# Row factors of the first blocks, side units, late finishes, query loads and the last scaling of a hybrid encoder layer: five placements changed

## The chip, the cores and the metric

The kernel runs on one core of one Trainium2 chip. The core has a matmul engine (PE, with its weight loads PEld), a vector engine (DVE), an activation engine (ACT), a general engine (POOL) and a queue engine (SP); DMAs are issued by SP, POOL and ACT. The metric is device microseconds of one execution, and a kernel's time is the median of its runs.

## The reference

One layer works on a sequence of 4096 rows of width 1024, all in float32. Cut to what matters:

```
hn   = rms_norm(x, norm_w)
proj = hn @ w_in                     # q,k,v,o,z and gates of group A; q,k,v,z of group B
qk_a = silu(conv5(qk_a) + conv_b)    # depthwise, centred
# group A, 4 heads x 128: a scan over chunks of 128 rows, once forward, once backward
#   s   = (q k^T) * exp(dmat - m);  num = s v + w * (q C);  den = sum(s) + w * (q n)
#   h   = num / max(|den|, exp(-m));  C = decay * C + (w k)^T v
h    = sigmoid(o) * (h_fwd + h_bwd)
h    = h * rsqrt(mean(h*h) + eps) * mhn_w * silu(z)
# group B, 8 query heads / 2 kv heads x 64: attention within |i-j| <= 128, bias table, sink
y_b  = attention(q, k, v) * silu(z_b)
out  = rms_norm(x + concat(h, y_b) @ w_out, final_norm_w)
```

## The kernel before, in words

The program has four stages that follow each other on PE. Matmuls take each float32 operand as a rounded high part and a low part, so a product is three matmuls (low times high, high times low, high times high). Products with the gate and the output weights are formed with seven block products instead of eight, which needs sums of blocks of rows and of weights made ahead.

`pass1` (lines 161 to 678) goes over 16 blocks of 256 rows. Each block's row factor 1/rms is worked out from the rows (ACT squares, DVE, then a power on POOL) and stored to the small DRAM tensor `rs_d`, 128 values of 4 bytes per store, by `keep_rows` (line 177, issued by POOL). For blocks 3 to 15, `spread` (line 260, issued by SP) reads a block's 256 factors back as a row on all partitions, `scale_raw` (line 265, POOL) multiplies the transposed input with them, ACT casts the high part (line 274) and POOL subtracts (line 275). Blocks 0 to 2 are normalised from their rows directly (`norm_now`, `norm_both`, `norm`); their factors are only kept in `KEPT` and stored for pass 2. The attention of group B runs interleaved: scores, transposes, and the weighted sum `op` (line 424), evicted to the one buffer `ab` by ACT (line 436) and DVE (line 437) and stored to `at_d` (line 439). Near the end of pass 1 a last list of pieces carries hooks at given positions; hook 1 held the stores of `KEPT`.

`pass2` goes over eight blocks `b` of 512 rows, from 7 down to 0. For each block it makes the values (`v2p`, line 999), then keys (parts `m` 4 to 7) and queries (`m` 0 to 3) of the four heads (`up`, line 1026); each part is copied by ACT, convolved with one ACT and four DVE instructions (lines 1043, 1045) and finished by a tanh on ACT, a DVE product (lines 1049, 1050) and a store. A finish can be put off into `c.late[m]` and called later in the stream. Keys are transposed (`ktp`, line 1091, psum tag "b" with two buffers), copied by ACT and DVE (lines 1093, 1094), and multiplied with the weighted values (`kv`, lines 151 to 153). The split input of the next block, eight tiles `xb` of 514 KB, is loaded by SP (line 861) while the last query part of the present one runs. Beside this run "side units" that prepare the sums for the seven-product form: `punit` (input blocks 0 to 2, which needs the row factors in `rs_d`), `sunit` and `wunit` (weights). Each has four steps: load, sums, low part, store. `side(b)` is called 16 times in a block, eight times in the value projections and eight times in the key projections, and starts unit `z` at given calls with steps 0, 3, 5 and 6 calls later.

`pass3` walks over 32 chunks. Per chunk PE does 42 matmuls of a gate stream (`P`, line 1332) with the scan's own work in fixed places between: `heads` (`num`, lines 1468, 1469), `scores` (`S`, line 1444) of the next chunk, the transpose of the finished chunk (`yout`, line 1503). DVE evicts the products (`o`, `z`, lines 1313 to 1323), and does `W` times `q` (line 1458), the decayed scores `E` (line 1446) and, last of a chunk, four products with the factor `ss` (line 1496), which POOL's power (line 1494) delivers. The chunk's inputs are loaded by SP two chunks ahead (`load_scan`); the gate stream's raw sums are loaded by `raw` (line 1271).

`tail` makes the output projection and the final norm.

The order on PE is the order in which the program is written. On the other engines and in the DMA queues a planner orders instructions by a simulated time line and by priority; `issue_after` (helper `behind`) puts an instruction behind a given one of its engine. Each engine executes its list in order, so an instruction that waits holds up all behind it. Tiles come from pools with a fixed number of buffers: `xtile` has 14 of 4 KB per partition, `c.slot` has 20 of about 2 KB.

Of the kernel before, what the change touches and what calls it, by code (L numbers as in the profile page):

```python
# [20 lines left out]
NH = 4  # L21
# [139 lines left out]
def pass1(c):  # L161
    nc, tc, A = c.nc, c.tc, c.A
    NB = 16
    with ExitStack() as es:
# [446 lines left out]

        norm_now(0)
# [58 lines left out]
        hooks.append((1, lambda: [keep_rows(b, i, r) for (b, i), r in KEPT.items()]))  # L671
# [199 lines left out]
def pass2(c):  # L871
    nc, tc, A = c.nc, c.tc, c.A
    with ExitStack() as es:
# [78 lines left out]
        def punit(b):  # L952
            T = {}

            def load():
                T["x"] = [xtile(c, [128, 4, 256], F32, f"xs{b}_{h}") for h in range(2)]
                T["r"] = c.slot([128, 256], F32, f"rs{b}")
                for h in range(2):
                    nc.gpsimd.dma_start(T["x"][h], A["xt"][b, :, 4 * h:4 * h + 4, :])
                nc.gpsimd.dma_start(T["r"], c.rs_d[b].partition_broadcast(128))  # L960

            def scale():
                for x in T["x"]:
                    nc.vector.tensor_tensor(out=x, in0=x, in1=T["r"].unsqueeze(1).broadcast_to([128, 4, 256]), op=ALU.mult)

            def store():
                for h in range(2):
                    nc.gpsimd.dma_start(c.xo_d[b, h], T["x"][h])

            return load, scale, lambda: block_sums(nc.vector, T["x"]), store  # L970
# [7 lines left out]
        def side(b):  # L978
# [6 lines left out]
            for z, u in enumerate(SIDE[b][1]):  # L985
                for d, f in zip((0, 3, 5, 6), u):
                    if ((0, 2, 5, 8) if b > 3 else (0, 4, 8))[z] + d == t:
                        f()
# [22 lines left out]
        def qkproj(b, m):  # L1011
# [6 lines left out]
            def unit(lo, hi, k, j):  # L1018
# [38 lines left out]
                if m == 7 or m == 0 and 0 < b < 7 or m == 3 and b:  # L1057
# [79 lines left out]
        for b in range(7, -1, -1):  # L1137
# [45 lines left out]
            if 0 < b < 7:  # L1183
# [79 lines left out]
def gate_stream(c):  # L1263
# [23 lines left out]
    def pair(j):  # L1287
# [49 lines left out]
        def ahead(i):  # L1337
            if i < 6:
                split(j, i + 1)
            plan = [(2, whole, j, 5), (3, whole, j, 6), (4, whole, j + 1, 0), (5, raw, j + 1, 3), (6, raw, j + 1, 2)]  # L1340
# [65 lines left out]
def pass3(c):  # L1406
    nc, tc, A = c.nc, c.tc, c.A
    with ExitStack() as es:
# [3 lines left out]
        Ls, OZ, TZ, HS, NUM = c.Ls, c.OZ, c.TZ, {}, {}  # L1412
# [47 lines left out]
        def heads(n, h):  # L1460
# [34 lines left out]
            for h in range(NH):  # L1495
                nc.vector.scalar_tensor_tensor(hs[:, h, :], hs[:, h, :], ss[:, h:h + 1], zs[:, h, :],
                                               ALU.mult, ALU.mult)
# [30 lines left out]
        for n in range(NCH):  # L1528
            m = n + 1
            with behind(c, c.rawd if n == 0 else None):  # L1530
                load(n + 2, ("cc", "e", "w", "q"))
# [17 lines left out]
            if m < NCH:  # L1549
                pieces.append(lambda: (scores(m), load(n + 2, ("k",))))  # L1550
                pieces.append(lambda: None)
            else:
                pieces += [lambda: None] * 6 + [lambda: yout(n)] + [lambda: None] * 2
# [350 lines left out]
```

## Time and profile before

| what | value |
|---|---|
| runs (us) | 2209.07, 2199.22, 2204.91; median 2204.91 |
| profiled execution | 2198.4 us, its span 2196.7 us |
| PE busy | 2129.6 us (97% of the span) |
| DVE, ACT, POOL busy | 1552.0, 1139.0, 715.5 us |
| mean granted PE clock | 0.994 |
| bytes moved | 460.72 MB, mean 210 GB/s |

In the profile, busy times are sums of instruction durations on an engine, and a line such as "PE a L1 <- DVE b L2: 5.0, 3, 2.1" says that PE's instruction of line 1 waited for DVE's of line 2, 5.0 us in total, 3 times, 2.1 us at the longest. A row of the time line gives start, duration, engine, line, operation, output and inputs, count, and in brackets the engine's idle time before it with what ended it. A row of windows gives the stretch, each engine's busy time with the instruction count, the granted clock, the share of the DMA engines and GB/s.

### The profile page before, as it was taken

To read this page: it belongs to the slowest core of one execution; us is meant where nothing else is said; L and a number is where in the kernel's file an instruction comes from. 1 tells how busy PE (TensorE), PEld (TensorE's weight loads), DVE (VectorE), ACT (ScalarE), POOL (GpSimd) and SP (SyncE) were. 2 spreads that over 40 slices of the span, in tenths; PEclk is the share of its full clock that TensorE was granted. 3 is DMA by queue.
4 is the path that set the end of the run, shared out by engine and by line. 5 is a ranking of instruction groups with operands and counts; after the bars stand their busy time and mean duration, and the time that the engine had idled before them with its cause. 6 is when DMAs were issued, how large, how long until landed. Compare 5 with 4: busy or idle time off the path is not lost.

```text
span 2196.7 us, 35248 instructions
## 1 busy us (share of the span) xinstructions
PE 2129.6 (97%) x12034; PEld 1843.2 (84%) x12034; DVE 1552.0 (71%) x3195; ACT 1139.0 (52%) x2764; POOL 715.5 (33%) x1055
## 2 busy tenths in 40 slices
PE   7899999999989999999999999999999999999998
PEld 7899999999888787788888788888888788888886
DVE  6677777778876775767765777777777543867776
ACT  6688888878644443444443455555555321333333
POOL 3565766653014233312410232332232111112222
PEclk9999999999999999999999999999999999999999
DMA  9665655533227546634666988888779998667765
GB/s 263 170 179 156 199 151 190 175 114 116 71 84 256 191 151 220 230 127 144 224 201 237 334 260 259 266 267 280 252 253 308 335 356 288 185 179 191 193 187 149
DMA packets 285762, 460.72 MB, mean 210 GB/s; under 512 B 23180, under 2 KB 151180, under 8 KB 284045
## 3 DMA queue, kind: packets, MB, share of 16 engines
q1 hardware_dynamic: 246016, 323.94, 46.4%
q0 software_dynamic: 39328, 134.25, 20.2%
q8 instruction: 95, 1.56, 0.3%
q14 instruction: 87, 0.70, 0.1%
q10 hardware_dynamic: 236, 0.27, 0.1%
HBM read 305.20 MB, written 153.17 MB: 209 GB/s over the span
## 4 chain that ended last, share of the span: by engine, by line
PE 64%; DMA 13%; DVE 8%; issue 7%; ACT 4%; POOL 3%; SPq 1%; POOLq 0%; ACTq 0%; DVEq 0%
PE up L1026 14%; PE P L1332 9%; PE qp L547 7%; PE v2p L999 5%; DMA xr<-x 5%; PE op L424 4%; PE tp L410 3%; PE zbp L151 3%; PE sp L379 3%; PE zbp L153 3%; PE zbp L152 3%; DMA xb<-xT_d 2%; PE o L1670 2%; PE num L1469 2%; PE num L1468 2%
## 5 line engine op out<-in xcount | busy, mean ns | idle before, releaser
L1332 PE MATMUL P<-wt,op 128*128 128x512 f32 x1344 | 364.1, 407 | 6.2 <-DVE o L1313 4.4
L1026 PE MATMUL up<-xb,w 128*128 128x512 f32 x1344 | 334.4, 396 | 0.0
L1670 PE MATMUL o<-wo,yo 128*128 128x512 f32 (+1 forms) x1356 | 312.7, 393 | 0.0
L1670 PEld LDWEIGHTS o<-wo,yo 128*128 128x128 f32 x1356 | 253.3, 188 | 59.5
L1026 PEld LDWEIGHTS up<-xb,w 128*128 128x128 f32 x1344 | 245.0, 188 | 48.5
L1332 PEld LDWEIGHTS P<-wt,op 128*128 128x128 f32 x1344 | 237.0, 189 | 53.1 <-issue 9.1
L1045 DVE SCALAR_TENSOR_TENSOR qk<-U,cw,qk 128x512 f32<-128x512 f32 x256 | 194.8, 761 | 82.5 <-ACT qk L1043 72.6
L547 PE MATMUL qp<-xT,wqb 128*128 128x256 f32 x1536 | 242.8, 288 | 0.1
L547 PEld LDWEIGHTS qp<-xT,wqb 128*128 128x128 f32 x1536 | 214.6, 190 | 8.4 <-DVE wqb L320 0.5
L413 DVE TENSOR_TENSOR pt<-tp,pt 128x512 fp32r<-128x512 f32 x188 | 129.6, 690 | 65.9 <-ACT pt L412 65.2
L999 PE MATMUL v2p<-w,xb 128*128 128x512 f32 x672 | 161.8, 401 | 8.7 <-DMA xb<-xT_d 7.2
L390 ACT ACTIVATE s<-s,NG 128x320 f32<-128x320 f32 (+1 forms) x256 | 142.2, 556 | 50.9 <-DVE NG L382 49.5
L382 DVE CUSTOM_DVE_ANT_0 s<-sp,G,nsink 128x320 f32<-128x320 f32 (+1 forms) x256 | 138.0, 539 | 38.7 <-PE sp L379 33.8
L999 PEld LDWEIGHTS v2p<-w,xb 128*128 128x128 f32 x672 | 128.1, 191 | 41.1 <-DMA xb<-xT_d 8.9
L412 ACT CAST pt<-tp 128x512 fp32r<-128x512 f32 x188 | 109.9, 584 | 44.0 <-PE tp L410 18.7
L424 PE MATMUL op<-pt,v 128*128 128x512 f32 x376 | 122.0, 406 | 10.8 <-DVE ab L437 10.0
L1483 ACT ACTIVATE hs<-num,r 128x128 f32<-128x128 f32 x128 | 46.8, 366 | 151.9 <-DVE r L1480 72.5
L379 PE MATMUL sp<-kk,q 128*128 128x320 f32 (+2 forms) x512 | 119.1, 313 | 1.6 <-DVE kk L500 1.0
L410 PE MATMUL tp<-ident,s 128*128 128x128 f32 x752 | 113.4, 273 | 1.9 <-DVE pt L413 1.9
L151 PE MATMUL zbp<-xc,w 128*128 128x512 f32 x256 | 102.1, 399 | 2.5 <-DVE az L1395 1.4
L1049 ACT ACTIVATE th<-qk 128x512 f32<-128x512 f32 x64 | 40.5, 632 | 117.4 <-DVE qk L1045 117.3
L153 PE MATMUL zbp<-xc,w 128*128 128x512 f32 x256 | 101.0, 395 | 0.0
(306 smaller groups left out, 4604.7 us busy)
## 6 DMA issues: line engine op xcount, KB each, us to landing
xc<-xT_d SPq DMA_DIRECT2D x64, 512.0 KB, 7.7
xT_d<-xT POOLq DMA_DIRECT2D x52, 512.0 KB, 7.9
xb<-xT_d SPq DMA_DIRECT2D x48, 514.0 KB, 7.9
op<-xT_d SPq DMA_DIRECT2D x96, 256.0 KB, 5.0
E<-m_d SPq DMA_DIRECT2D x64, 256.0 KB, 6.1
W<-w_d SPq DMA_DIRECT2D x64, 256.0 KB, 6.6
y<-y_d SPq DMA_DIRECT2D x32, 512.0 KB, 3.4
out<-xr POOLq DMA_DIRECT2D x31, 512.0 KB, 5.3
```

Of the source, the lines that this page charges most:

```text
L151: nc.tensor.matmul(out, wl, xh, start=first, stop=False)
L153: nc.tensor.matmul(out, wh, xh, start=False, stop=last)
L379: nc.tensor.matmul(sp[:, lo:hi], qt, kk[:, kv, z, col - 128 + lo:col - 128 + hi], start=(z == 0), stop=(z == 1))
L390: LAST["act"] = nc.scalar.activation(ps[g][:, kept(g)], ps[g][:, kept(g)], AF.Exp, scale=-1.0, bias=ng[:, g:g + 1], accum_out=rs[:, g:g + 1])
L410: nc.tensor.transpose(tp[:, g * 128:(g + 1) * 128], ps[g][:, j * 128:(j + 1) * 128], c.ident)
L424: nc.tensor.matmul(op, vt, pt[:, z, :], start=(i == 0 and z == 0), stop=(i == len(js) - 1 and z == 1))
L547: nc.tensor.matmul(qp, wq[k // 2][:, k % 2, w, m * 128:m * 128 + 128], x[k], start=(k == 0 and j == 0), stop=(k == KT - 1 and j == 2))
L999: nc.tensor.matmul(vp, a, wv[k // 2][:, k % 2, m, :], start=(k == 0 and j == 0), stop=(k == KT - 1 and j == 2))
L1026: nc.tensor.matmul(up[:, 0:hi - lo], w[k // 2][:, k % 2, a, cs], x, start=(k == 0 and j == 0), stop=(k == KT - 1 and j == 2))
L1045: nc.vector.scalar_tensor_tensor(acc, U[:, t:t + 512], cw[:, cm, t:t + 1], acc, ALU.mult, ALU.add)
L1332: nc.tensor.matmul(P[i], OPS[j, i][:, k, z, :], c.wt[i][k][m], start=k == 0 and a == 0, stop=k == 3 and a == 2)
L1670: nc.tensor.matmul(p, a[:, z, k, :], w[k // 2][:, k % 2, m, lo:hi], start=k == 0 and z == 1, stop=k == 3 and z == 0 and m == 0)
```

## The change

- `KEPT` stores: the six stores of blocks 0 to 2 are issued by SP instead of POOL, behind the attention store that is last at hook 8 of the closing list of pass 1.
- `punit`: its tile of row factors comes from the 14 `xtile` buffers instead of the 20 slots.
- `side`: the steps come 0, 3, 4 and 5 calls after a unit's start; units start at calls 0, 0, 4, 6 in blocks 6 to 4 (before: 0, 2, 5, 8) and at 0, 0, 3 in blocks 3 to 1 (before: 0, 4, 8).
- the finish of query part 0 of block 7 is put off to 39/96 of the stream of key transposes, as in the other blocks.
- `raw` loads of the gate stream come one product earlier from the second pair on.
- the last scaling of a chunk becomes a function `last` kept in `FIN`, called behind the second product of the next chunk's decayed scores; for the last chunk it is called in the piece after `heads`.
- the queries of chunk n+3 are loaded at the end of step n, behind the scores, instead of at the start of step n+1, behind `cc`, `e` and `w`.

```diff
--- before.py
+++ after.py
@@ -608,6 +608,11 @@
         def run(units):
             for u in units:
                 u()
+
+        def keep_first():
+            with behind(c, LAST["at"]):
+                for (b, i), r in KEPT.items():
+                    nc.sync.dma_start(c.rs_d[b].rearrange("(i p) -> p i", i=2)[:, i:i + 1], r)
 
         norm_now(0)
         for i, (ks, u) in enumerate(zip(((0, 1, 2), (3,), (4, 5), (6, 7)), transposes(0))):
@@ -668,7 +673,7 @@
         pieces += [(lambda i=i: att_o(2 * NCH - 1, i)) for i in range(3)]
         hooks = [(2 + 6 * i, lambda i=i: w2_piece(i)) for i in range(16)]
         hooks += [(p, lambda i=i: gate1(c, wk, i)) for i, p in enumerate((52, 54, 55, 57, 58, 60, 64))]
-        hooks.append((1, lambda: [keep_rows(b, i, r) for (b, i), r in KEPT.items()]))
+        hooks.append((8, keep_first))
         hooks.sort(key=lambda h: h[0])
         hooks += [(100, lambda: gate2(c, wk)), (113, lambda: gate3(c, wk))]
         for p, f in hooks[::-1]:
@@ -954,7 +959,7 @@
 
             def load():
                 T["x"] = [xtile(c, [128, 4, 256], F32, f"xs{b}_{h}") for h in range(2)]
-                T["r"] = c.slot([128, 256], F32, f"rs{b}")
+                T["r"] = xtile(c, [128, 256], F32, f"rs{b}")
                 for h in range(2):
                     nc.gpsimd.dma_start(T["x"][h], A["xt"][b, :, 4 * h:4 * h + 4, :])
                 nc.gpsimd.dma_start(T["r"], c.rs_d[b].partition_broadcast(128))
@@ -983,8 +988,8 @@
             t = SIDE[b][0]
             SIDE[b][0] += 1
             for z, u in enumerate(SIDE[b][1]):
-                for d, f in zip((0, 3, 5, 6), u):
-                    if ((0, 2, 5, 8) if b > 3 else (0, 4, 8))[z] + d == t:
+                for d, f in zip((0, 3, 4, 5), u):
+                    if ((0, 0, 4, 6) if b > 3 else (0, 0, 3))[z] + d == t:
                         f()
 
         def vproj(n):
@@ -1054,7 +1059,7 @@
                     if m >= 4:
                         KTS[b, h] = acc
 
-                if m == 7 or m == 0 and 0 < b < 7 or m == 3 and b:
+                if m == 7 or m in (0, 3) and b:
                     c.late[m] = finish
                 else:
                     finish()
@@ -1180,7 +1185,7 @@
 
             at = [((8, 16, 28, 38)[h] / 96, lambda h=h, b=b: ktp(b, h)) for h in range(NH)]
             at.append((17 / 96, lambda: c.late[7]()))
-            if 0 < b < 7:
+            if b:
                 at.append((39 / 96, lambda: c.late[0]()))
             k0 = 44 if b == 7 else 34
             at += [((k0 + (96 - k0) * (4 * (n3 - n) + hh) / 16) / 96, lambda n=n, hh=hh: kvp(n, hh))
@@ -1337,7 +1342,7 @@
         def ahead(i):
             if i < 6:
                 split(j, i + 1)
-            plan = [(2, whole, j, 5), (3, whole, j, 6), (4, whole, j + 1, 0), (5, raw, j + 1, 3), (6, raw, j + 1, 2)]
+            plan = [(2, whole, j, 5), (3, whole, j, 6), (4, whole, j + 1, 0), (4, raw, j + 1, 3), (5, raw, j + 1, 2)]
             if j == 0:
                 plan = [(3, whole, 0, 5), (4, whole, 1, 0), (4, raw, 1, 3), (5, raw, 1, 2)]
             elif j == 1:
@@ -1409,7 +1414,7 @@
         wk = c.p23
         c.psum({"pj": 3, "n": 2, "c": 1})
 
-        Ls, OZ, TZ, HS, NUM = c.Ls, c.OZ, c.TZ, {}, {}
+        Ls, OZ, TZ, HS, NUM, FIN = c.Ls, c.OZ, c.TZ, {}, {}, {}
 
         def small(tag, bufs, name):
             return c.slot([128, NH, 128], F32, name)
@@ -1492,9 +1497,13 @@
                 TZ["sq"] = nc.scalar.activation(jk, hs[:, h, :], AF.Square, accum_out=ss[:, h:h + 1])
             nc.vector.tensor_scalar(ss, ss, 1.0 / 128, 4 * EPS, ALU.mult, ALU.add)
             nc.gpsimd.tensor_tensor(out=ss, in0=ss, in1=c.nhalf, op=ALU.pow)
-            for h in range(NH):
-                nc.vector.scalar_tensor_tensor(hs[:, h, :], hs[:, h, :], ss[:, h:h + 1], zs[:, h, :],
-                                               ALU.mult, ALU.mult)
+
+            def last():
+                for h in range(NH):
+                    nc.vector.scalar_tensor_tensor(hs[:, h, :], hs[:, h, :], ss[:, h:h + 1], zs[:, h, :],
+                                                   ALU.mult, ALU.mult)
+
+            FIN[n] = last
 
         def yout(n):
             hs = HS.pop(n)
@@ -1528,7 +1537,9 @@
         for n in range(NCH):
             m = n + 1
             with behind(c, c.rawd if n == 0 else None):
-                load(n + 2, ("cc", "e", "w", "q"))
+                load(n + 2, ("cc", "e", "w"))
+                if n == 0:
+                    load(2, ("q",))
             if n + 2 < NCH:
                 state(m)
             with behind(c, c.rawd if n == 0 else None):
@@ -1547,10 +1558,14 @@
             if n:
                 pieces.append(lambda: yout(n - 1))
             if m < NCH:
-                pieces.append(lambda: (scores(m), load(n + 2, ("k",))))
-                pieces.append(lambda: None)
+                def ends():
+                    with behind(c, c.em):
+                        FIN.pop(n)()
+
+                pieces.append(lambda: (scores(m), load(n + 2, ("k",)), load(n + 3, ("q",))))
+                pieces.append(ends)
             else:
-                pieces += [lambda: None] * 6 + [lambda: yout(n)] + [lambda: None] * 2
+                pieces += [lambda: FIN.pop(n)()] + [lambda: None] * 5 + [lambda: yout(n)] + [lambda: None] * 2
             if n == NCH - 3:
                 for at, i in ((1, 0), (5, 1), (8, 2)):
                     pieces.insert(at, lambda i=i: zweights(i))
```

## The prediction

> **What bounds the kernel now.** I read the page's head first, then the list of PE's waits, then windows around the longest of them.
>
> ```profile
> span 2196.7 us, 35248 instructions
> PE 2129.6 (97%) x12034; PEld 1843.2 (84%) x12034; DVE 1552.0 (71%) x3195; ACT 1139.0 (52%) x2764; POOL 715.5 (33%) x1055
> ```
>
> PE is busy for all but 67 us, and the change takes no instruction from PE. What it can win is therefore part of those 67 us, and the time in which PE runs at a lower clock after a stall. The list of PE's waits says where they are (total, times, longest):
>
> ```profile
> PE op L424 <- DVE ab L437: 10.0, 9, 5.7
> PE v2p L999 <- DMA xb<-xT_d: 7.2, 4, 3.3
> PE ktp L1091 <- DVE kt L1094: 7.0, 5, 2.0
> PE kv L151 <- DVE kt L1094: 4.9, 1, 4.9
> ...
> PE P L1332 <- DVE o L1313: 4.4, 8, 1.4
> ...
> PE P L1332 <- DVE z L1320: 1.8, 2, 1.2
> PE v2p L999 <- ACT v L1005: 1.5, 1, 1.5
> ```
>
> Each longer stall costs more than its idle time. In the windows (PE busy is the first number after the length, the granted clock the one after POOL) stand the two longest stalls with what follows, and what follows two of the xb waits:
>
> ```profile
> 76.00:82.00 6.00, 0.28 (x3) 0.18 (x2) 0.90 (x2) 2.65 (x5) 5.07 (x3) 0.82 0.24 84
> 82.00:87.00 5.00, 5.00 (x21) 4.68 (x22) 4.28 (x12) 4.93 (x16) 5.00 (x6) 0.54 0.67 216
> ...
> 646.50:651.50 5.00, 0.06 (x2) 0.08 (x1) 4.98 (x7) 2.53 (x6) 1.72 (x5) 0.83 0.09 27
> 651.50:656.70 5.20, 5.20 (x24) 5.20 (x25) 1.39 (x4) 2.10 (x5) 0.19 (x1) 0.51 0.10 28
> ...
> 762.00:766.00 4.00, 3.96 (x10) 3.13 (x11) 3.32 (x4) 2.60 (x5) 0.36 (x1) 0.57 0.28 105
> ...
> 843.00:848.00 5.00, 4.88 (x14) 3.89 (x15) 4.41 (x7) 3.23 (x6) 0.57 (x1) 0.66 0.25 96
> ```
>
> A stretch of length t at clock c loses t(1-c): 2.3, 2.5, 1.7 and 1.7 us. The two long stalls thus cost 5.7+2.3 = 8.0 and 4.9+2.5 = 7.4 us, the xb waits 7.2+3.4 = 10.6.
>
> **Part 1, the stores of the first factors.** Each is a POOL instruction and a train of 4-byte writes on POOL's queue. The early time line of POOL shows block 2's two ahead of those of block 3, for which everything then waits:
>
> ```profile
> 48.16 1.14 POOL L177 DMA_DIRECT2D rs_d<-rstd  x2
> ...
> 52.26 1.11 POOL L177 DMA_DIRECT2D rs_d<-rstd  x2
> ```
>
> SP, ACT and PE then show the consequence (SP's wait in total, its load, the landing times of line 177's stores in the first 80 us, and the scaling, its cast and PE behind it):
>
> ```profile
> SPq L260 <- DMA rs_d<-rstd: 11.6, 1, 11.6
> ...
> 69.31 0.33 SPq L260 DMA_DIRECT2D rsb<-rs_d  x1
> ...
> DMA to landing us min/median/max: 9.7/10.3/11.0
> ...
> 76.93 4.64 POOL L265 TENSOR_TENSOR xraw<-xraw,rsb 128x1024 f32<-128x1024 f32 x2 [12.37 <-issue]
> ...
> 79.30 1.14 ACT L274 CAST xT<-xraw 128x512 fp32r<-128x512 f32 x2 [6.25 <-POOL xraw L265]
> ...
> 81.82 1.22 PE L424 MATMUL op<-pt,v 128*128 128x512 f32 x2 [5.72 <-DVE ab L437]
> ```
>
> Block 3's second store is issued at 52.8 and its reader starts only at 69.31, 16.5 us later, where the other stores of this stretch take 9.7 to 11.0 us: it queues behind block 2's. Without those, POOL comes 1.14 us sooner (51.7) and the store lands after some 11 us, at 62.7, 6.6 us earlier. The scaling then starts at 70.3, ACT's cast at about 72.7 instead of 79.30, and `ab` is ready near 75.2, before PE asks at 76.1. I take the whole 8.0 us. Bounds: 0 (other traffic keeps the store late) and -8.0.
>
> The six stores come back on SP. Nearest in form are its scattered issues, and there is room at the new place, where SP's next attention store waits through a gap:
>
> ```profile
> 27.26 3.78 SPq L350 DMA_DIRECT2D G<-bv_d  x4
> ...
> 477.98 19.00 SPq L439 DMA_DIRECT2D at_d<-ab  x2
> 480.00:500.00 20.00, 19.90 (x149) 19.03 (x149) 15.02 (x39) 15.97 (x42) 7.29 (x8) 1.00 0.24 79
> ```
>
> Six at 3.78/4 = 0.95 us are 5.7 us of issue inside the 19 us between two attention stores, with the DMA engines at 0.24: cost 0. Were that cover gone, the attention store behind them would hold the single buffer `ab` up to 5.7 us longer, which is the other bound. The readers come only in pass 2. The Trainium skill (DMA: Bandwidth & Descriptors, Issuing engines are not separate DMA queues) says that DMAs of every issuing engine share the same 16 DMA engines, so a change of issuer alone saves only issue time. By that rule this part would be worth the 1.14 us of POOL unless the later moment counts. Here the moment moves by over 400 us, and the trace's 16.5 against 11 us puts the price on the place in the queue.
>
> **Part 2, block 7's late finish.** The stall at 646.5 waits for the third and fourth transposed keys. Their casts stand on ACT behind the tanh of query part 0, and their subtractions on DVE behind its product:
>
> ```profile
> 647.31 0.63 ACT L1049 ACTIVATE th<-qk 128x512 f32<-128x512 f32 x1
> ...
> 648.59 1.50 DVE L1050 SCALAR_TENSOR_TENSOR qk<-th,qk 128x512 f32<-128x512 f32 x1
> 650.02 0.68 DVE L1104 TENSOR_TENSOR wvr<-v2t,TM 128x516 f32<-128x516 f32 x1
> 650.62 1.28 DVE L1094 TENSOR_TENSOR kt<-ktp,kt 128x512 fp32r<-128x512 f32 x2
> ```
>
> Put off to behind the fourth transpose, these two no longer stand ahead. DVE gets to the keys at least 1.5 us sooner, plus part of ACT's 0.6: 1.9 us. The shorter stall, about 3 us, then resembles the one ahead of 843, which loses 1.7 instead of 2.5. Together -2.7; bounds 0 (the weighting of line 1104 stays the last) and -7.4. What is late next is the product itself, wanted only in pass 3. The Trainium skill (TensorE: Matmul & The Clock Gate, What's actually happening) lets the clock halve only after an idle window of about 3.4 us. By that rule the remaining stall would cost no clock and this part would give 4.4; no wait for xb was longer than 3.3 us and the clock still fell to 0.57 and 0.66 behind two of them, so the sum goes by the trace.
>
> **Part 3, side units.** Their instructions and bytes stay the same; places change. (a) Sums end by call 10 instead of 13, so DVE and ACT carry less in the key projections. In blocks 6 to 4 the fourth key transpose waits for the third's cast, which the planner put behind a copy of `kv`:
>
> ```profile
> PE ktp L1091 <- DVE kt L1094: 4.0, 3, 1.3
> ...
> 808.29 0.27 ACT L1127 COPY kf<-kv 128x129 f32<-128x129 f32 x1 [1.08 <-PE kv L153]
> ...
> 809.18 0.58 ACT L1093 CAST kt<-ktp 128x512 fp32r<-128x512 f32 x1
> ```
>
> Blocks 3 to 1, with three units instead of four, have no such wait. The order comes from the planner's picture of that load, which I can't know: half, -2.0; bounds 0 and -4.0. (b) Loads come earlier. At the start of a block xb already competes:
>
> ```profile
> 735.00:762.00 27.00, 25.08 (x126) 20.79 (x124) 18.02 (x35) 10.18 (x23) 12.31 (x26) 1.00 0.99 321
> ...
> 972.00:997.00 25.00, 25.00 (x127) 21.03 (x126) 18.41 (x38) 11.68 (x26) 12.63 (x26) 1.00 0.98 328
> wu<-w_in POOLq DMA_DIRECT2D x32, 128.0 KB, 5.8
> ```
>
> The engines are full (0.98 to 0.99) in a block with xb waits and in one without. A weight unit loads two times 128 KB, so one more ahead of the last xb costs 0.26 MB / 321 GB/s = 0.8 us. Against that, buffers free up no sooner and gate the loads, and the factors' tile no longer waits for a slot. I take +1.0. Bounds: two more weight units and the factors (0.66 MB, 2.1 us) ahead of xb in all six blocks, 12.6, plus 1.7 of clock in the four blocks that don't pay it now, 6.8: +19.4; and all waits of line 999 with their clock gone, 10.6+1.5: -12.1.
>
> **Part 4, the scan.** The waits in its stretch, and one case of them on DVE and PE:
>
> ```profile
> DVE hs L1496 <- POOL ss L1494: 49.8, 28, 4.6
> ...
> DVE W L1458 <- DMA lq<-q_d: 26.1, 21, 2.9
> ...
> 1497.67 1.14 DVE L1496 SCALAR_TENSOR_TENSOR hs<-hs,ss,z 128x128 f32<-128x128 f32 x4 [4.60 <-POOL ss L1494]
> ...
> 1501.34 0.96 PE L1332 MATMUL P<-wt,op 128*128 128x512 f32 x3 [1.20 <-DVE z L1320]
> ```
>
> DVE stands 4.60 us for POOL's power; behind it wait the evictions, and PE, with three psum buffers, loses 1.20. So 75.9 us of DVE waiting reach PE as the 4.4+1.8 = 6.2 us of the list. The change puts the four products behind the decayed scores, when the power is long done, and loads the queries ahead of three other loads. I take -4.0 of the 6.2. What stays behind the new place is the next chunk's reciprocals, and the chunk's transpose a good half step later. SP's new order and the earlier raw loads can hold up the decays' loads; as a DVE stand of 4.6 us costs PE 1.2, I bound that by two more such stands: +2.4. The other bound is -6.2.
>
> **The sum.** -8.0 - 2.7 - 2.0 + 1.0 - 4.0 = -15.7 from the profiled execution's 2198.4 gives 2182.7. The median of the runs is 6.5 above that execution, so a median of 2189.2: 2189, a gain of 0.7%.
>
> **The rivals.** *The early stall stays.* Block 3's store must pass DMA engines that are full anyway, and the stores of block 2 were only part of its delay. For it: it needs 5.7 of the 6.6 us that I expect. Against: 16.5 us against 11. Time: 2189+8 = 2197.
>
> *Side loads starve xb: slower.* The price is 19.4 instead of 1.0, so 2189+18.4 = 2207. It decides as soon as part 3b costs more than the other parts bring, 16.7 us, or 2.8 per block in six blocks. For it: the full DMA engines at each block's start. Against: the loads wait for buffers, which the change doesn't add; the factors even take one.
>
> *Block starts clear up.* Casts and sums no longer wait for late side loads and xb lands in time: -12.1 instead of +1.0, so 2176. For it: the 1.5 us wait for ACT's `v`, whose list holds a side cast. Against: those full engines.
>
> **How the numbers follow.** Chances: forecast 0.55, early stall 0.20, starving 0.13, clearing 0.12. The forecast's own range, from parts 2, 3a and 4 at their ends, is 2180 to 2200; the whole reaches to 2174 and 2206 for the two outer cases. About 0.5% (11 us) is what a measurement of this kernel can tell from no change. Below 2194 lie about 0.73 of the forecast's chance and all of the clearing case: 0.53. Above 2216 I leave 0.07, for starving worse than priced. The rest, 0.40, is the same.
>
> **What would show it.** Part 1 is right if PE's wait for `ab` falls to about 4 us and the clock stays at 1 from 76 to 87; wrong if SP still waits some 11 us for `rs_d`. Part 2: PE's wait for `kt` in `kv` under 3.5 us. Part 3: the waits for `kt` gone in blocks 6 to 4, and those for xb no longer than now; more of them make the forecast wrong. Part 4: DVE's wait for POOL's power near zero, PE's P waits under 2.5 us. If the P waits grow, SP's order has become the new hold.

## The result, and the profile after

| what | before | after |
|---|---|---|
| median of the runs (us) | 2202.74 | 2192.63 |
| profiled execution (us) | 2198.4 | 2192.97 |

The ratio is 0.9951, with a 95% interval of 0.9931 to 0.9971: a gain of 0.5%, on the border of what a measurement of this kernel can tell. One of the six runs of before was a slow one (3492.43 us); the ratio leaves it out, and without it before's median is 2200.57. The forecast was 2189, in a range of 2174 to 2206.

The page's head of the kernel after shows the same 12034 matmuls:

```profile
span 2191.2 us, 35245 instructions
PE 2126.5 (97%) x12034; PEld 1839.1 (84%) x12034; DVE 1544.2 (70%) x3195; ACT 1139.0 (52%) x2764; POOL 710.6 (32%) x1049
```

Where the time went shows when the span is cut at PE's own borders: the first `up` (end of `pass1`), the first `v2p` that reads `xb` (end of block 7), the first `S`, the first `zbp` (end of the scan). Windows of before, then of after. The second number is the length, then PE's busy time; the granted clock stands behind the five engines:

```profile
0.00:603.90 603.90, 578.38 (x4228) 548.78 (x4229) 456.30 (x1119) 465.86 (x1193) 310.14 (x437) 0.99 0.55 162
603.90:671.90 68.00, 60.27 (x468) 58.09 (x466) 43.37 (x73) 29.09 (x65) 14.07 (x30) 0.95 0.42 135
671.90:1232.70 560.80, 543.77 (x2542) 446.43 (x2541) 383.12 (x598) 235.58 (x435) 159.75 (x308) 0.99 0.61 200
1232.70:1685.60 452.90, 446.21 (x2593) 383.37 (x2593) 341.28 (x856) 245.14 (x760) 134.54 (x148) 1.00 0.84 271
```
```profile
0.00:602.40 602.40, 578.41 (x4228) 548.88 (x4229) 455.13 (x1119) 465.19 (x1193) 307.20 (x431) 0.99 0.53 162
602.40:663.40 61.00, 58.18 (x468) 55.94 (x467) 42.17 (x70) 28.39 (x62) 14.05 (x29) 1.00 0.45 144
663.40:1216.20 552.80, 540.64 (x2542) 444.10 (x2540) 384.65 (x600) 237.12 (x438) 159.78 (x309) 1.00 0.61 204
1216.20:1679.80 463.60, 448.42 (x2593) 383.76 (x2593) 334.72 (x856) 245.01 (x760) 132.80 (x148) 1.00 0.81 264
```

So `pass1` gains 1.5 us, block 7 gains 7.0, the other seven blocks of `pass2` gain 8.0, and the scan loses 10.7. The tail stays within 0.3. A gain of 16.5 in the first two passes is mostly given back in the scan, where PE's busy time for the same matmuls rises by 2.2 us (446.2 to 448.4) and its idle time by 8.5 (6.7 to 15.2).

PE's waits after, in the order of their size (lines 1337, 1096, 1004 answer to 1332, 1091, 999 of before):

```profile
PE P L1337 <- DVE z L1325: 11.6, 12, 1.9
PE op L424 <- DVE ab L437: 9.4, 10, 3.0
PE ktp L1096 <- DVE kt L1099: 7.7, 5, 2.1
...
PE v2p L1004 <- DMA xb<-xT_d: 2.2, 3, 1.3
PE sp L379 <- DVE NG L382: 2.2, 1, 2.2
PE P L1337 <- DVE o L1318: 2.1, 5, 1.1
```

The wait of `kv` for the keys (4.9) is gone, those for `xb` fell from 7.2 to 2.2, those for the keys' transposes did not fall, and the waits of the gate stream `P` rose from 6.2 to 13.7. The wait of `sp` for `NG` grew from 0.6 to 2.2.

### The profile page after: what moved, and what is told of

The parts are those of the page before. It is cut to its first block, busy times and chain, and to the rows that moved or that the text cites. A ratio compares the mean times of both kernels' runs of the same rounds, so it can differ in the third digit from the quotient of the medians.

```text
span 2191.2 us, 35245 instructions
## 1 busy us (share of the span) xinstructions
PE 2126.5 (97%) x12034; PEld 1839.1 (84%) x12034; DVE 1544.2 (70%) x3195; ACT 1139.0 (52%) x2764; POOL 710.6 (32%) x1049
## 4 chain that ended last, share of the span: by engine, by line
PE 60%; DMA 14%; DVE 10%; issue 7%; ACT 5%; POOL 3%; SPq 1%; POOLq 0%; ACTq 0%; DVEq 0%
PE up L1031 13%; PE qp L547 8%; PE P L1337 6%; PE v2p L1004 6%; DMA xr<-x 5%; PE op L424 3%; PE tp L410 3%; DMA E<-m_d 3%; PE sp L379 3%; PE zbp L151 3%; PE zbp L153 3%; PE zbp L152 3%; DMA xb<-xT_d 2%; DMA W<-w_d 2%; PE num L1474 1%
## 5 line engine op out<-in xcount | busy, mean ns | idle before, releaser
L1337 PE MATMUL P<-wt,op 128*128 128x512 f32 x1344 | 365.7, 407 | 14.0 <-DVE z L1325 11.6
L424 PE MATMUL op<-pt,v 128*128 128x512 f32 x376 | 122.0, 406 | 10.2 <-DVE ab L437 9.4
L151 PE MATMUL zbp<-xc,w 128*128 128x512 f32 x256 | 102.4, 400 | 2.6 <-DVE az L1400 1.4
L1503 DVE SCALAR_TENSOR_TENSOR hs<-hs,ss,z 128x128 f32<-128x128 f32 x128 | 46.5, 424 | 79.8 <-POOL ss L1499 79.8
```

Of the source, the lines that this page charges most:

```text
L151: nc.tensor.matmul(out, wl, xh, start=first, stop=False)
L424: nc.tensor.matmul(op, vt, pt[:, z, :], start=(i == 0 and z == 0), stop=(i == len(js) - 1 and z == 1))
L1337: nc.tensor.matmul(P[i], OPS[j, i][:, k, z, :], c.wt[i][k][m], start=k == 0 and a == 0, stop=k == 3 and a == 2)
```

## The experiments

Each diff is against the changed kernel unless the text says otherwise. Where a kernel's time is one execution, the verdict rests on its trace's stages and waits, since executions of the kernel before on one chip lie between 2188 and 2198. A difference of 3 us between two such stages, in pass 1 of 5, is itself within their scatter, as is shown below; the waits say more. "Scan" is the stretch from the first `S` to the first `zbp`, "pass 1" that up to the first `up`, as above.

### Block 7's late finish: undone, and alone

Undone:

```diff
-                if m == 7 or m in (0, 3) and b:
+                if m == 7 or m == 0 and 0 < b < 7 or m == 3 and b:
...
-            if b:
+            if 0 < b < 7:
```

> The changed kernel with the finish of query part 0 of block 7 at its old place, at once. Theory (tanh and product ahead of the key casts): PE's wait of kv for kt returns, 4.9 us, with half clock from about 650 to 656, 2.5 us: 2200. Rival (side steps cleared it): the stall stays under 1 us and the time at 2193.

Measured 2198.54 us (before on the same chip: 2196.37). PE's wait is back at its old size, in its old place:

```profile
PE kv L151 <- DVE kt L1099: 4.9, 1, 4.9
```

Block 7 takes 67.7 us again instead of 61.0, and in and behind the wait the clock again loses what 6.8 us at one half lose, as before.

Alone, that is the kernel before with these two lines of the change (its last scaling of a chunk is also put into a function, which is called at once):

```diff
-                if m == 7 or m == 0 and 0 < b < 7 or m == 3 and b:
+                if m == 7 or m in (0, 3) and b:
...
-            if 0 < b < 7:
+            if b:
```

> The kernel before with one edit alone, the late finish of query part 0 of block 7. Theory (that stall also set the phase of the block starts): the kv stall of 4.9 us and its half clock go (7 us) and the xb waits and their half clock shrink as they did with the old side units (by 5 to 9 us): 2196.4 - 12 to 16, so 2181 to 2185. Rival (the side edits cleared the block starts by themselves): xb waits stay near 7 us with their half clock, 2189.

Measured 2190.30 us (before: 2194.57). Block 7 takes 61.0 us. PE's wait for the keys in `kv`, and that for `xb` in the other blocks:

```profile
PE v2p L999 <- DMA xb<-xT_d: 5.0, 3, 2.6
...
PE kv L151 <- DVE kt L1094: 0.4, 1, 0.4
```

Where the stall went shows in the cast of the third head's keys on ACT, first before, then with the late finish alone:

```profile
647.85 0.57 ACT L1093 CAST kt<-ktp 128x512 fp32r<-128x512 f32 x1
```
```profile
641.64 0.58 ACT L1093 CAST kt<-ktp 128x512 fp32r<-128x512 f32 x1
```

The transpose that it reads ends on PE at 640.4 before and at 639.4 here, so the cast comes 7.4 us and 2.3 us behind it. Before, three instructions of ACT stood ahead of the cast: a cast of weighted values, for which ACT was idle for 3.11 us until DVE delivered them, a copy and the tanh (647.31). With the tanh put off, the planner placed the keys' casts ahead of that other cast as well, and DVE's first subtraction moved from 650.62 to 644.65.

What follows: the late finish alone takes 7 us out of block 7, the whole stall with its clock, and needs nothing else of the change. The 2181 to 2185 us that were expected did not come: the waits for `xb` shrank only from 7.2 to 5.0.

### The side units undone

```diff
-                T["r"] = xtile(c, [128, 256], F32, f"rs{b}")
+                T["r"] = c.slot([128, 256], F32, f"rs{b}")
...
-                for d, f in zip((0, 3, 4, 5), u):
-                    if ((0, 0, 4, 6) if b > 3 else (0, 0, 3))[z] + d == t:
+                for d, f in zip((0, 3, 5, 6), u):
+                    if ((0, 2, 5, 8) if b > 3 else (0, 4, 8))[z] + d == t:
```

> The changed kernel with the side units at their old calls and steps and the factors' tile of punit back in a slot. Theory (side work holds block starts): waits of the value products for xb return from 2.2 to about 7 us and half-clock windows appear after two of them, 3.4 us: 2193 + 5 + 3 = 2201. Rival (phase): xb came in time because block 7 no longer stalls; then xb waits stay under 3.5 us and the time within 2 us of 2193.

Measured 2190.91 us (before: 2196.37; the changed kernel 2192.63 in its own runs). The other seven blocks take 554.5 us, 1.7 more than in the changed kernel, but the nine other kernels here that share its second pass take 551.8 to 555.5, so these 1.7 us are no cost that can be told. The waits are much the same:

```profile
PE ktp L1096 <- DVE kt L1099: 6.8, 5, 2.0
...
PE v2p L1004 <- DMA xb<-xT_d: 2.3, 3, 0.9
```

The waits of the key transposes are 6.8 here, 7.0 before, and 7.7 with the new places of the sums: moving the sums out of the key projections does not touch them. The waits for `xb` stay low without the new places too. They were 7.2 before, 5.0 with the late finish alone, 2.5 with all but the late finish, 3.0 with all but the stores' move, and 2.3 with all but the side units: no single part is needed to clear them. Neither the theory nor the rival's reason holds, since they stay low with block 7's stall back too. Which transfer it is that now lets `xb` land in time stays open, and so does whether the 7.2, from the one trace of before, were in part chance.

### The six stores: back on POOL, early

```diff
-        hooks.append((8, keep_first))
+        hooks.append((1, lambda: [keep_rows(b, i, r) for (b, i), r in KEPT.items()]))
```

> The changed kernel with the six stores of the first row factors back on POOL at hook 1. Theory (SP's queue): on SP the six stores, 768 writes of 4 bytes, stand right ahead of a weight load for which ACT then waits 5.2 us, and PE loses 2.2 + 1.4 us with the clock halved from 523.9 to 530.7. Undone, those two waits and that half clock go, some 6 us, and the first long stall of before comes back (5.7 us at 76 and half clock to 87, against 3.0 us and one half-clock window of 3.4 us in the changed kernel), some 4 us: about 2 us faster than the changed kernel's 2192.97, so 2191. Rival (the planner): another order of the closing list makes the waits at 520, not the stores; then PE still waits over 1.5 us for NG near 520.

Measured 2196.81 us (before: 2196.37), not the 2191 expected: pass 1 takes 605.7 us. PE's stall near 77 us is 6.0 again. Near 515 us no engine waits long for an output weight: ACT's waits for `w2s` from 455 to 600 us come to 0.7 us in total, and 0.2 in the kernel before. In the changed kernel they come to 5.2. So the stores cost something in either place, and the trace of the changed kernel shows both.

In the kernel before, the program has these stores near the end of pass 1, but the planner issued them from 7 to 49 us, the last two right ahead of block 3's.

What is left at the early place in the changed kernel: PE's and SP's longest waits from 40 to 95 us, then rows of SP's and ACT's time line, then the window behind the stall:

```profile
PE op L424 <- DVE ab L437: 3.0, 1, 3.0
...
SPq L260 <- DMA rs_d<-rstd: 26.8, 2, 17.0
```
```profile
53.76 0.33 SPq L260 DMA_DIRECT2D rsb<-rs_d  x1
...
72.12 0.33 SPq L439 DMA_DIRECT2D at_d<-ab  x1
...
82.12 0.58 ACT L436 COPY ab<-op 64x512 f32<-64x512 f32 x1 [3.62 <-DMA at_d<-ab]
```
```profile
82.00:87.00 5.00, 3.52 (x14) 3.34 (x15) 3.65 (x10) 3.75 (x11) 2.56 (x10) 0.66 0.91 311
```

Block 3's factors are read at 53.76 instead of 69.31, so they are no longer what PE waits for. The queue of stores is not the whole of it. The second store of block 3 is issued at 45.79 in the changed kernel and at 52.84 before, and 7.1 of the 15.5 us are that. With the stores back early it is issued at 52.78 and its reader starts at 64.24, 11.5 us later and not 16.5, although the stores of block 2 stand ahead of it again; but then the read itself takes 14.3 us to land, beside block 4's two stores (64.91), against 4.9 in the changed kernel. From the issue of that store to the scaling 24.1 us pass before and 25.9 in this run, and to the landing of the read 12.8 in the changed kernel. So the early stores double that time, and whether the store or the read is late differs from trace to trace. What is late next is the attention store: issued at 72.12, beside two more factor stores of POOL (71.45), it gives `ab` free only at 82.12, 10 us later, and PE loses 3.0 us and then part of its clock (0.66).

The late place in the changed kernel, in the time lines of SP, ACT and PE, then in two windows:

```profile
506.24 2.81 SPq L615 DMA_DIRECT2D rs_d<-rstd  x6
509.15 2.21 SPq L575 DMA_DIRECT2D w2s<-w_in  x2
...
519.76 1.37 ACT L696 ACTIVATE w<-w2s,nw 128x512 fp32r<-128x512 f32 x2 [5.21 <-DMA w2s<-w_in]
...
521.91 0.56 PE L379 MATMUL sp<-kk,q 128*128 128x320 f32 x2 [2.19 <-DVE NG L382]
...
526.86 1.22 PE L424 MATMUL op<-pt,v 128*128 128x512 f32 x2 [1.36 <-DVE ab L437]
```
```profile
519.70:523.90 4.20, 1.79 (x13) 1.56 (x13) 3.32 (x8) 3.98 (x10) 0.00 (x0) 1.00 0.24 67
523.90:530.70 6.80, 5.44 (x23) 4.95 (x22) 4.79 (x12) 4.22 (x11) 0.00 (x0) 0.50 0.35 108
```

The stores did not go where the prediction put them, into the gap at 478. They left at 506.24, ahead of loads of the output weights, not of an attention store. ACT stood 5.21 us for a weight, the attention's casts and maxima stood behind it, PE lost 2.19 and 1.36 us, and ran 6.8 us at half clock.

### The six stores on POOL, at the same late hook

```diff
-            with behind(c, LAST["at"]):
+            with behind(c, LAST["pool"]):
                 for (b, i), r in KEPT.items():
-                    nc.sync.dma_start(c.rs_d[b].rearrange("(i p) -> p i", i=2)[:, i:i + 1], r)
+                    nc.gpsimd.dma_start(c.rs_d[b].rearrange("(i p) -> p i", i=2)[:, i:i + 1], r)
```

> The changed kernel with the six stores of the first row factors at the same hook, but issued by POOL behind its last block work instead of by SP. Theory (SP's queue): the 768 small writes now wait in POOL's queue, where nothing is behind them that PE needs soon; the weight load's landing falls from 10.6 us to 3 to 5, ACT's wait for it from 5.2 us to under 1, PE's wait for NG near 520 goes, pass 1 ends 4 to 6 us sooner than 602.4: 2187 to 2189. Rival (the small writes slow every transfer, whichever queue): ACT still waits over 3 us for the weight load and PE over 1 us, time 2191 to 2193.

Measured 2193.0 us (before: 2195.93). The longest waits of ACT and PE near 515 us, and the landing times of the two weight loads that SP issued at 504.8 and 505.3:

```profile
ACT w L696 <- DMA w2s<-w_in: 6.8, 1, 6.8
PE op L424 <- DVE ab L437: 5.5, 1, 5.5
```
```profile
DMA to landing us min/median/max: 10.1/10.2/10.2
```

POOL issued the six stores from 499.6 on, on its own queue, and the loads on SP's queue took 10.2 us all the same. In the seven kernels with the stores on SP at this hook, the weight load behind them that has a landing time took 8.9 to 9.4 us. It is not the place on SP that holds the weights up but the 768 writes of 4 bytes themselves. The Trainium skill (DMA: Bandwidth & Descriptors, Issuing engines are not separate DMA queues) says that the transfers of all issuing engines interleave on the same DMA engines; this run agrees, with 10.2 us behind POOL's stores.

### The scan's edits undone, together and one by one

All three undone at once (each of the three diffs below):

> The changed kernel with the scan's three edits undone (last scaling at once, queries loaded at the start of a step, raw sums one product later). Theory (the edits delay the decays' loads, so POOL's power and DVE stand longer): PE's P waits fall from 13.7 back to about 6.2 us and DVE's wait for POOL's power from 75.7 to about 50: 2185.5. Rival (a shifted phase of the scan, from the earlier parts): the P waits stay above 11 us and the time at 2193.

Measured 2180.48 us (before: 2196.37). The scan takes 456.2 us instead of 463.6, `P` waits 4.3 + 3.2 us, DVE waits 58.3 for the power in the whole program instead of 79.8.

Only the query loads undone:

```diff
-                load(n + 2, ("cc", "e", "w"))
-                if n == 0:
-                    load(2, ("q",))
+                load(n + 2, ("cc", "e", "w", "q"))
...
-                pieces.append(lambda: (scores(m), load(n + 2, ("k",)), load(n + 3, ("q",))))
+                pieces.append(lambda: (scores(m), load(n + 2, ("k",))))
```

> The changed kernel with only the query loads back at the start of a step. Theory (queries between the decays' loads): without a query load between the two halves of E, POOL's second mask stands 1 to 2 us less, the power comes sooner, DVE's wait for it falls from 75.7 to about 50 us and PE's P waits from 13.7 to about 6 to 8: 2185. Rival (raw sums or late scaling do it): P waits stay over 11 us, time 2193.

Only the last scaling back in its old place (`last()` called at once instead of kept in `FIN`):

```diff
-            FIN[n] = last
+            last()
...
-                    with behind(c, c.em):
-                        FIN.pop(n)()
```

> The changed kernel with only the last scaling back at once behind POOL's power. Theory (queries between the decays' loads): the new place of the scaling does nothing, since the decayed scores already stand ahead of it on DVE; P waits stay near 13.7 us, DVE's wait for the power near 75 us, time 2192 to 2194. Rival (the late scaling holds DVE and the z slots): P waits fall to 6 to 8 us, time 2185.

Only the raw loads undone (the end of one line):

```diff
-(4, raw, j + 1, 3), (5, raw, j + 1, 2)]
+(5, raw, j + 1, 3), (6, raw, j + 1, 2)]
```

> The changed kernel with only the raw sums' loads back one product later. Theory (queries between the decays' loads): no change, P waits 12 to 15 us, 2193. Rival (raw loads take buffers and DMA time from the decays' loads): P waits fall to 6 to 8 us, 2185.

| undone | time (us) | scan (us) | P waits (z + o, us) |
|---|---|---|---|
| nothing | 2192.63 | 463.6 | 11.6 + 2.1 |
| raw loads | 2192.37 | 463.7 | 11.3 + 1.1 |
| last scaling | 2187.02 | 460.9 | 8.7 + 3.2 |
| query loads | 2184.42 | 457.1 | 3.3 + 4.1 |
| all three | 2180.48 | 456.2 | 3.2 + 4.3 |
| (kernel before) | 2202.74 | 452.9 | 1.8 + 4.4 |

The first and the last time are medians, the others single executions; before took 2194.57 and 2196.37 beside them. The query loads carry the loss. For the other two the scan's time decides nothing: five kernels that have the changed scan take 461.8 to 464.3 us, so the 2.7 us of the late scaling are little more than scatter, and with the raw loads undone the scan also ran at a clock of 0.98 from 1300 to 1400 and from 1600 us to its end, which cost it 3.6 us and could hide a gain of that size. By their `P` waits, 11.9 and 12.4 us against 13.7, each is worth 1 or 2 us at most. How a load on SP makes DVE wait for POOL is seen in one chunk. Rows of the time lines of SP, POOL, DVE and PE after:

```profile
1537.49 0.56 SPq L1265 DMA_DIRECT2D E<-m_d  x1
1538.15 0.72 SPq L1256 DMA_DIRECT2D lq<-q_d  x1
1538.92 0.47 SPq L1265 DMA_DIRECT2D E<-m_d  x1
...
1538.08 1.28 DVE L1451 TENSOR_TENSOR E<-S,E 128x512 f32<-128x512 f32 x2
...
1541.87 0.16 DVE L1498 TENSOR_SCALAR ss<-ss 128x4 f32<-128x4 f32 x1
...
1546.71 0.64 POOL L1437 TENSOR_SCALAR_AFFINE_SELECT E<-E 128x512 f32<-128x512 f32 x1 [2.42 <-DMA E<-m_d]
1547.31 1.05 POOL L1499 TENSOR_TENSOR ss<-ss,nhalf 128x4 f32<-128x4 f32 x1
...
1548.39 1.14 DVE L1503 SCALAR_TENSOR_TENSOR hs<-hs,ss,z 128x128 f32<-128x128 f32 x4 [6.37 <-POOL ss L1499]
...
1552.06 0.96 PE L1337 MATMUL P<-wt,op 128*128 128x512 f32 x3 [1.91 <-DVE z L1325]
```

With the query loads in their old place, SP issues the two halves of those decays together, and the query 3.4 us later:

```profile
1531.22 1.04 SPq L1265 DMA_DIRECT2D E<-m_d  x2
```

DVE's wait for the power in the scan, first with the query loads undone, then in the changed kernel:

```profile
DVE hs L1503 <- POOL ss L1499: 51.5, 27, 3.5
```
```profile
DVE hs L1503 <- POOL ss L1499: 75.7, 27, 6.4
```

In the changed kernel the planner moved the query load between the two halves of the decays `E` of a later chunk. POOL masks each half as it lands, and the power `ss` stands behind the second mask. So the power is late, DVE stands 6.37 us for it, and PE 1.91 us behind DVE's evictions. The rows of DVE also show why the scaling's own new place wins nothing: the next chunk's scores `E` are done at 1539.4, ahead of the power's input (line 1498), so the scaling still follows that input directly, as before (1489.12 `E`, 1492.91 input, 1497.67 scaling).

Counted over the scan of the changed kernel: in 13 of 32 chunks the query load stands between the halves, and there the power ends 4.6 us after its input on average (the end of line 1499 less the end of line 1498); in the other chunks 1.2 us after it. The same 13 chunks show 2.5 us with the query loads undone and 2.3 in the kernel before, so a split makes the power some 2 us later. With the query loads or all three edits undone, no chunk has the split. With only the scaling undone the 13 splits stay, with 4.2 us.

### Stores on POOL and the scan's edits undone; with the power put first

The first of the two joins the edits "stores on POOL, at the same late hook" and "all three undone":

> The changed kernel with the stores on POOL's queue at hook 8 and the scan's three edits undone; the late finish and the side edits stay. Theory: pass 1 ends near 597, the scan takes 456 as in the run with the scan edits undone: 2179 to 2182, 0.5 to 0.7% below the changed kernel and 0.9 to 1.1% below the kernel before. Rival (the gain of the run with the scan undone was a lucky phase of the clock's windows): 2184 to 2188 in the median.

Measured 2185.07 us (2182.43 to 2187.50), before 2195.93: a ratio of 0.995, 0.9936 to 0.9964. The time lies where the rival had it, and the expected 597 us of pass 1 did not come. Pass 1 takes 603.4 us and the scan 455.7: the scan's edits are undone, but the stores on POOL still make ACT wait 6.8 us for a weight and PE 5.6 us behind it.

The second also puts POOL's masks of the next chunk's decays behind the present chunk's power:

```diff
-            nc.gpsimd.tensor_tensor(out=ss, in0=ss, in1=c.nhalf, op=ALU.pow)
+            c.pow = nc.gpsimd.tensor_tensor(out=ss, in0=ss, in1=c.nhalf, op=ALU.pow)
...
-                nc.gpsimd.affine_select(out=e[:, d], in_=e[:, d], compare_op=ALU.is_ge, fill=BIG, base=0,
+                with behind(c, c.pow):
+                    nc.gpsimd.affine_select(out=e[:, d], in_=e[:, d], compare_op=ALU.is_ge, fill=BIG, base=0,
```

> As the run before it, with one edit more in the scan: on POOL the masks of the next decays stand behind the power of the present chunk, so that the power no longer waits for the loads of E. Theory (the power behind E's loads is what holds DVE): DVE's wait for the power falls from some 52 us to some 35 (about 1.2 us each), PE's P waits from 7.5 to under 4, the scan by 3 to 5 us: 2176. Rival (the masks then come late, and with them the decayed scores and PE's products with E): the P waits fall but PE waits for E, the scan takes 456 or more and the time is 2180 or more.

Measured 2202.7 us (2199.26 to 2206.99), a ratio of 1.003 to before, 1.0019 to 1.0041. Waits of POOL, ACT and PE in its scan:

```profile
POOL ss L1500 <- DVE ss L1499: 152.6, 27, 6.3
...
ACT E L1442 <- POOL E L1438: 57.9, 28, 3.8
...
PE P L1337 <- DVE z L1325: 21.0, 13, 2.7
```

DVE's wait for the power falls to 20.7 us in the whole program, but now POOL stands 152.6 us for the power's input and its masks come late: ACT waits 57.9 us for them, and `P` waits 21.0. POOL's order in the old scan is a compromise between power and masks, and the power first is the worse end of it.

### The six stores behind the last weight load, and the scan's edits undone

```diff
-        hooks.append((8, keep_first))
+        hooks.append((99, keep_first))
```

and the three diffs of the scan.

> The changed kernel with its three edits of the scan undone, and the six small stores still on SP but at hook 99, behind the last load of an output weight (hook 92), so no weight load stands behind their 768 writes. Theory (the small writes are what held up the weight load; the stall near 510 to 525 is theirs): ACT's wait for w2s near 505 to 545 falls from 5.2 us (SP, hook 8) and 6.8 us (POOL, hook 8) to under 1.5 us, PE's gaps of 2.2 and 1.4 us there go, and with them the 6.8 us of half clock, pass 1 takes about 598 us, the scan 456 us; median 2178 to 2182. Rival (a load of that stretch is late anyway, and the small writes only moved which one): ACT still waits 4 us or more for w2s, or PE's stall comes back behind hook 99 as a wait for another load (gate weights, xb of block 7), and the median stays at 2184 to 2188, with the version that has the stores on POOL at hook 8.

Measured **2178.89 us** (2175.44 to 2180.96), before 2194.54: a ratio of 0.9931, 0.9914 to 0.9949. The time lies in the 2178 to 2182 that the theory gave. It is faster than the kernel before, and its slowest run is below the fastest of the changed kernel (2188.41). These two were not run side by side, and their ratios to before, 0.9931 and 0.9951, have intervals that overlap. SP's stores leave at 575.6, behind the last weight load. The landing times, as far as the trace has them, of the four weight loads that SP issues from 500 to 520 us, ACT's wait for such loads, and the windows of pass 1 and the scan:

```profile
DMA to landing us min/median/max: 2.6/2.7/2.7
```
```profile
ACT w L696 <- DMA w2s<-w_in: 0.5, 1, 0.5
```
```profile
0.00:596.10 596.10, 575.39 (x4228) 546.20 (x4229) 454.34 (x1119) 465.39 (x1193) 307.88 (x431) 1.00 0.53 164
...
1209.60:1666.50 456.90, 448.97 (x2592) 384.78 (x2592) 339.66 (x856) 245.03 (x760) 133.88 (x148) 1.00 0.82 268
```

2.7 us for a weight instead of 10.2 with the stores beside it, no stall near 515, and pass 1 at 596.1 against 597.2 to 602.4 in the seven kernels with the stores on SP at hook 8: that place had cost some 4 us on their mean (600.0), 6 in the changed kernel's own trace. How much of this is the place and how much the luck of the clock is not settled. The kernel with only the scan's edits undone differs from this one in the place of the stores alone. There ACT waits 4.8 us for the weight and PE 1.7 us for `NG` and 2.0 for `ab`, without a lower clock, and its pass 1 (597.2) and its time (2180.48, one execution) are within 2 us of this kernel's. The scan's edits had cost 6.7.

## Why the prediction was right and wrong

The time came out in the range and 3.6 us from the forecast, but not by the forecast's own sum. That was made against before's profiled execution: 2182.7. The profiled execution after is 2192.97, 10.3 us above it. The 6.5 us by which the median then lay above the profiled execution covered most of this; after, median and profiled execution agree within 0.4. So that the number came close was in part luck: of the five terms only part 2 was right in its mechanism, two had the wrong sign, and the misses cancel in part. Term by term, in the order of the prediction:

**Part 1, -8.0 forecast, -1.5 measured between the two traces.** That the early stores make block 3's factors late was right: their read came 15.5 us earlier. That its store "queues behind block 2's" is not borne out as the reason, as the run with the early stores shows, and POOL came 7 us sooner, not 1.14. "I take the whole 8.0 us" failed: the next wait, for the attention store, was not looked for, and kept 3.0 us and 3.4 us of halved clock. By the prediction's own signs this part was wrong: PE's wait for `ab` is 9.4 us in all and not about 4, the clock falls to 0.66 from 82 to 87, and SP waits 26.8 us for `rs_d`. "Cost 0" for the six stores failed worse. The step priced only the 5.7 us of issue on SP (2.8 measured) and named the attention store as the cost if cover is gone; it priced neither the 768 small writes on the DMA engines nor what loads stand behind them. Over the kernels run, pass 1 takes 602.8 to 605.7 us with the stores early, 602.8 to 603.4 with them on POOL late, 597.2 to 602.4 with them on SP at hook 8, and 596.1 behind the weights. So the move can be worth some 8 us (604.1, the mean of the three early ones, less 596.1, which is one trace), as forecast, but only in the last of these places. The move as it was made gains 4.1 us on the means (604.1 less 600.0), more than the one pair of traces shows.

**Part 2, -2.7 forecast, -7.0 measured.** The mechanism held and the size was wrong. The step "at least 1.5 us sooner, plus part of ACT's 0.6: 1.9 us" counted the time that the product and the tanh themselves take, as if all else in the lists stayed in its place, and left a 3 us stall. But the planner also moved the keys' casts ahead of another cast, for which ACT had been waiting: they come 2.3 us behind the transpose instead of 7.4, the wait falls to 0.4 us with the late finish alone and is gone in the changed kernel. That all but reaches the outer bound of -7.4.

**Part 3a, -2.0 forecast, 0 measured.** The key transposes wait 7.7 us against 7.0. The side sums are not what makes them wait.

**Part 3b, +1.0 forecast, a gain measured.** The wrong sign: the waits for `xb` fell by 5.0 us, and with them the clock behind two of them. Together 3a and 3b give -8.0, as in the rival "block starts clear up" (-12.1 as an outer bound). The runs do not give this to the side units: without them it stays, but for 1.7 us within the scatter.

**Part 4, -4.0 forecast, +10.7 measured.** The step that failed is "The change puts the four products behind the decayed scores, when the power is long done". On DVE the next scores already stood ahead of the power's input, so the new place waits for the same power. And SP's new order made the power later still, in 13 of 32 chunks. The prediction named this way ("SP's new order and the earlier raw loads can hold up the decays' loads") and bounded it at two stands, +2.4; it came 13 times, each some 2 us of DVE's time. The last sign that it named was right: the `P` waits grew, and SP's order was the new hold. Of the 10.7, 7.4 come back when the three edits are undone. The remaining 3.3 don't: the scan takes 455.7 to 456.9 us in every kernel with its old edits whose earlier part was changed, late finish alone included, against 452.9 in the one trace of before. Why is open; some 2 us of it are waits (7.5 us of `P` and 2.2 of `S` with all three undone, 6.2 and 1.4 before).

The rival "side loads starve `xb`" fell. "The early stall stays" held in half: another wait took over at the same place.

## What to carry to other kernels

Price a moved DMA by its packets as well as by its issue: small stores belong where no load that somebody waits for is under way, on whichever queue. Read the wait behind the one that you remove before you book the whole stall, and when you move an instruction out of a planned list, expect the rest of the list to move too. And where a planner orders a queue, moving one load can split a pair of others; ask who waits for the second half.

## What the runs showed of the hardware

Six stores of 128 values of 4 bytes each made weight loads land after 8.9 to 10.2 us that took 2.6 to 2.7 with the stores put later. Issued by SP or by POOL, they held weights up: ACT stood 5.2 us for one in the first case, 6.8 in the other.

Here a clock that halves loses 1.7 us, as 3.4 us at one half do, or 3.4, as 6.8 us do, and much the same wait sometimes costs it and sometimes not. The wait for `ab` near 83 us is the plainest case, in three kernels whose pass 1 is the same program. It is 2.98 us with the side units undone, and the clock stays at 1.00 from 76 to 93 us; 3.00 in the changed kernel, with 0.66 from 82 to 87; and 3.02 with the raw loads undone, with 0.50 from 82 to 87 and 0.85 from 87 to 93. The first of them (the changed kernel's window stands above):

```profile
82.00:87.00 5.00, 4.29 (x31) 4.11 (x32) 3.61 (x11) 4.04 (x12) 0.82 (x5) 1.00 1.04 360
```

The other place: with waits of 2.19 and 1.36 us the changed kernel ran 6.8 us at 0.50 (above). With only the scan's edits undone, and so the same work up to there, the waits were 1.75 and 2.00 us, and the clock stays at 1.00 from 516 to 531.

That kernel's pass 1 took 597.2 us, 5.2 less than the changed kernel's, so differences of that size between single executions are not the edit's. The Trainium skill (TensorE: Matmul & The Clock Gate, What's actually happening) describes a free-running window of about 3.4 us, which agrees with the steps of 3.4 and 6.8 and with the luck. It also has the clock fall after at least one idle window; here PE was busy for 1.79 of the 4.20 us ahead of the halved clock, and its longest wait there was 2.19 us, which does not agree.
